# Moving w_out's first products into the attention's last steps of a two-layer encoder, with mLSTM and attention on one set of PSUM banks

## The chip, the cores and the metric

The kernel runs on one core of a Trainium2 chip. The metric is the device time of one execution in microseconds (us). TensorE does the matmuls into eight PSUM banks of 128 x 512 floats, VectorE (DVE), ScalarE (ACT) and GpSimd (POOL) the rest, and SyncE (SP) issues most DMAs.

## The reference

Two layers (`DEPTH = 2`) run over 512 rows of 1024 columns. In each layer one input projection feeds three kinds of heads side by side: eight heads of latent attention, four of a bidirectional chunked mLSTM, four of a bidirectional Mamba-2 SSD. Their outputs, put side by side, go through one output projection `w_out`, then come a layer norm, a mixture of experts (1 of 4 groups, 2 of its 4 experts a row) and a second layer norm:

```python
for l in range(DEPTH):
    p = jnp.einsum('bsd,dc->bsc', x, w_in[l])
    (c_q, c_kv, k_r, m_q, m_k, m_v, m_o, m_g, s_z, s_xbc, s_dt) = _split(p, IN_SIZES)
    y_a = _mla(c_q, c_kv, k_r, cos, sin, ...)
    y_b = _mlstm(m_q, m_k, m_v, m_o, m_g, ...)
    y_c = _ssd(s_z, s_xbc, s_dt, ...)
    heads = jnp.concatenate([y_a, y_b, y_c], -1)
    mix = jnp.einsum('bsc,cd->bsd', heads, w_out[l])
    x = _layernorm(DEEPNORM_ALPHA * x + mix, ln1_g[l], ln1_b[l])
    ffn = _hier_moe(x, ...)
    x = _layernorm(DEEPNORM_ALPHA * x + ffn, ln2_g[l], ln2_b[l])
```

The mLSTM's end matters here: its output `h` is normalised per head of 64 columns (mean, variance, inverse root) and multiplied by the sigmoid of `m_o`, the output gate.

## The kernel before, in words

All data of the run lie in 37 slots of SBUF of 128 x 1040 words (`Slots`, L100), which the code takes with `get` or, in halves, with `get_half`, and gives back with `free`. Free slots stand in a list, first in, first out. Free halves stand in one of their own: `get_half` takes the oldest free half, and cuts a new slot only where there is none; two free halves of a slot join again. Who gets which slot is settled when the program is written. An instruction that writes into a slot must wait on the chip until the last reader of that slot's former contents is done.

PSUM banks are handed out in the same way. Banks 0 to 2 (`PA`) hold projections, the attention's key and query products (`pk`, `pq`) and its outputs (`po_`). Of the other five, two belong to the mLSTM (`PM`) and three to the attention's scores and transposes (`PT_`), L253:

```python
PM, PT_ = Slots(banks[MA:MA + NM], 512), Slots(banks[NPA:MA] + banks[MA + NM:8], 512)
```

The mixing stage of a layer is a set of generators, each of which does one step when it is asked: `ssd` (d, L921, 19 steps), `projections` (p, L993), `mlstm` (m, L1066, 16 steps), `mla_in` (i, L1236), `ssd_heads` (h, L984), and the attention's `scores` (s) and `values` (v, from L1289). A head's `scores` are five steps: the q product, and a score tile with its softmax for each of four row tiles. The q product is six matmuls, a multiplication by the rotation table `rot` into a half slot (`qf`), and a split into a high and a low part. `values` are four steps of transposes, and for each second head two more with the products with v. One string, `SEQ` (L72), tells in which order the steps are asked for, a letter each. That settles the program order, and with it slots and banks. A planner then lays out each engine's queue, in program order where it can, and takes a later instruction first where by its model the earlier one isn't ready. On the chip each engine works through its queue in that order. All instructions of VectorE, ScalarE and TensorE go through one helper and carry the line L230; all loads have L277, POOL's splits L410, and POOL's normalisation of a probability tile L1338. In the trace `s` is any slot, `b` any bank, and `xt` one of the eight pairs of slots for x transposed and later for the heads' outputs.

The last two steps of `projections` are the two halves of the output gate: each is two row tiles of 24 matmuls with 256 columns, and leaves a half slot `tho`. The last step of `mlstm` does the normalisation, and its final reads of the gate free both halves:

```python
for i2 in range(2):
    hh = hb_.ap[:, i2 * 512:(i2 + 1) * 512]
    V.scalar_tensor_tensor(hh, tho[i2].ap, 1.0, hh, op0=OP.add, op1=OP.mult)
free(tho)
```

In `SEQ` the gate's halves stand before the SSD's last two steps and right behind them. `ssd_heads` (the split of the SSD heads' output) is asked for before the attention begins. The mLSTM's last step stands behind head 4's second score tile.

Behind the mixing stage comes w_out. Its weights come in eight tiles of 512 KB, four for the first 512 output columns, in the order `(3, 2, 0, 1)`: the columns of the SSD heads, of the mLSTM heads, then of the attention's. `wo_load` (L1623) loads one, `wo_split` (L1651) splits it into a high and a low part, ScalarE the one and VectorE or, for the pieces in `WOG = (0, 2)`, POOL the other. `wo_mm` (L1657) multiplies it for one row tile: six matmuls of 512 columns, 24 for the four row tiles, which add up in four banks of `P4` (banks 0 to 3). The code asks for all of it behind the attention; the planner may lay it further ahead.

Of the kernel before, what the change touches and what calls it, by code (L numbers as in the profile page):

```python
# [68 lines left out]
MA = 3  # L69
NM = 2  # L70
SSD_STEPS = 19
SEQ = 'dpddpdpdpddpdddpdpddpiddpidpiddpddphimmssmsmssmsvmsvvsmsvsmsmvssvsvvsvmmvsvsvsmvmsvsmsvmsvsvmvvsvmmsvsvsmssvvmsmsvsvmsvsvsvvssvsvvsvsvvvvvv'  # L72

ROPE_INV = [1.0, 0.5623413324356079, 0.3162277638912201, 0.17782793939113617, 0.10000000149011612,
            0.05623413249850273, 0.03162277489900589, 0.017782794311642647, 0.009999999776482582,
# [12 lines left out]
        'A n3 l2 c2 K23 Z0 o3 e3 b3 r3 r3 g3 r3 r3 l3 c3 f2 k2 K34 Z1 Z2 f3 H Z3')  # L88
WPIN = ''
NU = 7  # L90
WOG = (0, 2)
MG = (16, 16)
PTV = range(8)
GSEQ = 'gzgzgzgzzz'
# [118 lines left out]
def tile_trunk(ctx: ExitStack, tc: tile.TileContext, ins, out, dbg=None, depth=DEPTH):  # L213
# [36 lines left out]
    Q, R = View(pool, F32R), View(pool, F32)  # L250
    banks = [psp.tile([128, 512], F32, name=f"b{i}") for i in range(8)]
    PA, PB = Slots(banks[0:NPA], 512), Slots(banks[NPA:8], 512)
    PM, PT_ = Slots(banks[MA:MA + NM], 512), Slots(banks[NPA:MA] + banks[MA + NM:8], 512)  # L253
    lows_ = {}
    lastp, lows = ["pre"], {}

# [151 lines left out]
    def split(dst_h, dst_l, src, eng=V):  # L408
        r = A.activation(dst_h, src, AF.Copy)
        eng.tensor_sub(dst_l, src, dst_h.bitcast(F32))  # L410
        return r
# [147 lines left out]
    for l in range(depth):  # L559
# [361 lines left out]
        def ssd():  # L921
            for g in range(2):
                py = PB.get()
                cbs = []
                (_, ch, cl), (_, bh, bl) = cc_[g], bb_[g]
                for d in range(2):
                    bcs, bds = [], []
                    for e in range(2):
                        p = bcast(8 * d + 4 + 2 * g + e, PB)
                        bcs.append(p)  # L930
                        b = R.get_half()
                        V.tensor_tensor(b.v("p (a c) -> p a c", a=NT), p.v("p (a c) -> p a c", a=NT),
                                        (neg_u if d == 0 else neg_l)[:, None, :].to_broadcast([128, NT, 128]), op=OP.add)
                        bds.append(b)
                    for i in range(NT):
                        if d == 0:
                            pcb = PB.get()
                            s = slice(i * 128, (i + 1) * 128)
                            mm3(pcb.ap, bh[:, s], bl[:, s], ch, cl)
                            cb = R.get_half()  # L940
                            A.activation(cb.ap, pcb.ap, AF.Copy)
                            pcb.free()
                            cbs.append(cb)
                        lo_, hi_ = (i, NT) if d == 0 else (0, i + 1)
                        w = slice(lo_ * 128, hi_ * 128)
                        Ls = []
                        for e in range(2):
                            hd = 2 * g + e
                            L = R.get_half()
                            for c in range(lo_, hi_):  # L950
                                b = slice(c * 128, (c + 1) * 128)
                                src = bds[e] if c == i else bcs[e]
                                A.activation(L[:, b], src[:, b], AF.Exp, bias=sb[d][:, abs(c - i), i, hd:hd + 1])
                            V.tensor_mul(L[:, w], cbs[i][:, w], L[:, w])
                            Ls.append(L)
                        for e in range(2):
                            hd = 2 * g + e
                            T.matmul(py[64 * e:64 * e + 64, w], xdt[d][i][:, hd * 64:hd * 64 + 64], Ls[e][:, w],
                                     start=(d == 0 and i == 0), stop=(d == 1 and i == NT - 1), skip_group_check=True)
                        free(Ls)  # L960
                        yield
                    free(bcs, bds)
                free(cbs)
                y = R.get_half()
                V.scalar_tensor_tensor(y.ap, xs[g].ap, dsk[:, g:g + 1], py.ap, op0=OP.mult, op1=OP.add)
                py.free()
                V.tensor_mul(y.ap, y.ap, z2[g].ap)
                q = R.get_half()
                A.activation(q.ap, y.ap, AF.Square)
                yz.append(y)  # L970
                yq.append(q)
                free(cc_[g][0], bb_[g][0])
                yield
            free(xdb, xs, z2)
            r = rms_cols([[q.ap] for q in yq], 128.0, 4e-6)
            free(yq)
            for g in range(2):
                p = row_bc(r, g * NT)
                V.scalar_tensor_tensor(yz[g].ap, yz[g].ap, pt[:, 5 + g, 6:7], p.ap, op0=OP.mult, op1=OP.mult)
                p.free()  # L980
                tap("ssd%d_%d" % (l, g), yz[g].ap)
            yield

        def ssd_heads():  # L984
            for g in range(2):
                finish_heads(6 + g, yz[g].ap)
                yz[g].free()
            yield
# [247 lines left out]
        def mla_in():  # L1236
            for i in range(2):
                b, h, lo = pair()
                split(h[64:96], lo[64:96], kra[64:96])
                V.tensor_copy(h[96:128], h[64:96].bitcast(F32))  # L1240
                V.tensor_copy(lo[96:128], lo[64:96].bitcast(F32))
                kb.append((b, h, lo))
            kra.free()
            rq = rms_cols([[q.ap for _, q in cqb]], 256.0, 1e-6)

            qsc = small([128, 2, NT], tag="qsc")
            for c in range(2):
                V.tensor_scalar(qsc[:, c], rq, (1.0, -1.0)[c] * 96.0 ** -0.5, None, op0=OP.mult)
            qn = [c for c, _ in cqb]
            rk = rms_cols([[ckb[0][1].ap]], 128.0, 1e-6)  # L1250
            p = row_bc(rk, 0)
            c = ckb[0][0]
            V.scalar_tensor_tensor(c.ap, c.ap, pt[:, 2, 6:7], p.ap, op0=OP.mult, op1=OP.mult)
            p.free()
            kn = pair(c.ap)
            free(ckb[0][0], [b for _, b in cqb + ckb])
            yield
            ukv = R.get(1024)
            load(ukv.ap, ins["w_ukvp"], l * RANK_KV * 1024, [[1024, 128], [1, 1024]])
            uk = []  # L1260
            for w in range(2):
                b, h, lo = pair()
                split(h, lo, ukv[:, w * 512:(w + 1) * 512])
                uk.append((b, h, lo))
            ukv.free()
            yield
            vt = []
            for i in range(NT):
                s = slice(i * 128, (i + 1) * 128)
                p = PA.get()  # L1270
                mm3(p.ap, kn[1][:, s], kn[2][:, s], uk[1][1], uk[1][2])
                v = R.get_half()
                A.activation(v.ap, p.ap, AF.Copy)
                p.free()
                vt.append(v)
            uk[1][0].free()
            mla.update(qsc=qsc, qn=qn, kn=kn, uk=uk[0], vt=vt)
            router_sums()
            yield
# [110 lines left out]
                    if PHASE:  # L1390
                        print(t[2], "steps", t[0] - 1, "of", t[1])

        streams = {"d": ssd(), "p": projections(), "m": mlstm(), "i": mla_in(), "h": ssd_heads()}
        for n, t in enumerate(SEQ):
            ph({"m": "mlstm", "d": "ssd", "p": "proj"}.get(t, "attn"))
            if t == "s" and "s" not in streams:
                streams["s"], streams["v"] = attention()
            next(streams[t], 1)
        for t in "dphmisv":
            assert next(streams[t], 1) == 1  # L1400
        free([b for b, _, _ in kb], [b for b, _, _ in mla["qn"]], mla["kn"][0], mla["uk"][0], mla["vt"])


        P4, P5 = Slots(banks[0:4], 512), Slots(banks[4:8], 512)


        class Expert:
# [212 lines left out]

        ph("wout")

        def wo_load(hf, q):  # L1623
            raw = R.get(1024, full=True)
            load(raw.ap, ins["w_outp"], ((l * 2 + hf) * 4 + q) * 128 * 1024, [[1024, 128], [1, 1024]])
            return raw

        order = (3, 2, 0, 1)
        raws = [[wo_load(0, q) for q in order]]
        xr = load_x(ins["x"] if l == 0 else x2d)  # L1630
        ln1 = load_ln(1)
        lg = small([128, NT, 20], tag="lg")
# [3 lines left out]
        def ranks(a, b):  # L1636
# [10 lines left out]
            V.tensor_reduce(r1, gt4, axis=AX.X, op=OP.add)  # L1647
            V.tensor_sub(df[:, n], df[:, n], r1)
            gb_.free()

        def wo_split(raw, n):  # L1651
            h, lo = Q.get(1024, full=True), Q.get(1024, full=True)
            split(h.ap, lo.ap, raw.ap, G if n in WOG else V)
            raw.free()
            return h, lo

        def wo_mm(p, i, q, w, first, last):  # L1657
            s = slice(i * 128, (i + 1) * 128)
            for a in range(2):
                j = 2 * q + a  # L1660
                cc = slice(a * 512, a * 512 + 512)
                mm3(p.ap, xh[j][:, s], xl[j][:, s], w[0][:, cc], w[1][:, cc],
                    start=(first and a == 0), stop=(last and a == 1))

        def evac(p, i, hf):

# [19 lines left out]
            p.free()  # L1686

        lgt = [R.get_half(plain=True) for _ in range(2)]
        ps = [P4.get() for _ in range(NT)]
        for a, q in enumerate(order):  # L1690
            w = wo_split(raws[0][a], a)
            for i in range(NT):
                wo_mm(ps[i], i, q, w, a == 0, a == 3)
            free(w)
# [535 lines left out]
```

## Time and profile before

Three runs took 1066.09, 1066.67 and 1069.11 us. The profile is of one execution.

| | before |
|---|---|
| time, median of 3 runs | 1066.67 us |
| time of the profiled execution | 1070.26 us |
| span of the profiled execution | 1067.8 us |
| its mean granted TensorE clock | 0.974 |
| TensorE busy (matmuls) | 996.5 us, 93% |
| VectorE busy | 836.0 us, 78% |
| ScalarE busy | 644.6 us, 60% |
| GpSimd busy | 267.2 us, 25% |

The busy time of an engine is the sum over its instructions, its share is that of the span. The granted clock is what the chip allowed TensorE, as a share of 2.4 GHz; a stretch at 0.50 ran at 1.2 GHz. Times in views of the trace count from the start of the span. The mixing stage's part that the change touches lies from about 155 to 295 us in the first layer and from about 685 to 822 us in the second.

### The profile page before, as it was taken

Reading aid. Unit: us, or ns where it says so; the run is one execution under the profiler, and the core shown is the slowest. Engines: PE = TensorE matmul, PEld = TensorE weight load, DVE = VectorE, ACT = ScalarE, POOL = GpSimd, SP = SyncE. Lnnn points to the kernel's source line nnn. Section 1 sums busy time; section 2 is a strip of 40 time slices with the busy share of each in tenths; the row PEclk is TensorE's granted clock in tenths of the full one; section 3 lists DMA queues with packets and bytes.
Section 4 is the critical chain, followed back from the end, with each engine's and each line's share of the span. In section 5 each row is a group of like instructions: output and inputs, shape, how many; then the busy total and the mean of one; then the engine's idle time right before and its main releaser. Section 6 shows DMA issues by size and latency. Waiting matters only on the chain. (4 is left out here: it accounts for less than half of the span.)

```text
span 1067.8 us, 15553 instructions
## 1 busy us (share of the span) xinstructions
PE 996.5 (93%) x5310; PEld 739.2 (69%) x5310; DVE 836.0 (78%) x1832; ACT 644.6 (60%) x1182; POOL 267.2 (25%) x232
## 2 busy tenths in 40 slices
PE   6999999988998999999999999999799989999995
PEld 6876788555687666666598768876466876666653
DVE  8995557787749799999969955577876498999996
ACT  5565646555524588888646564466464347778874
POOL 1000002223003255565100000022220123556652
PEclk9999989998999899999999998999999989999998
DMA  7211100132656889996532120011347477999933
GB/s 305 69 45 45 40 21 21 35 126 99 234 198 218 282 288 345 335 324 213 204 139 70 40 69 1 21 40 41 118 138 246 168 275 264 311 339 337 308 94 155
DMA packets 51795, 176.76 MB, mean 166 GB/s; under 512 B 8169, under 2 KB 8681, under 8 KB 51712
## 3 DMA queue, kind: packets, MB, share of 16 engines
q1 hardware_dynamic: 45216, 160.42, 42.2%
q0 software_dynamic: 6496, 15.31, 6.0%
q8 instruction: 42, 0.69, 0.3%
q14 instruction: 41, 0.34, 0.1%
HBM read 159.61 MB, written 23.59 MB: 172 GB/s over the span
## 5 line engine op out<-in xcount | busy, mean ns | idle before, releaser
L230 PE MATMUL b<-xt,s 128*128 128x512 f32 (+3 forms) x1484 | 327.1, 367 | 13.8 <-ACT s L230 8.6
L230 PE MATMUL b<-s,s 128*128 128x512 f32 (+7 forms) x1308 | 324.7, 404 | 14.0 <-ACT s L230 7.1
L230 PEld LDWEIGHTS b<-xt,s 128*128 128x128 f32 (+2 forms) x1484 | 234.0, 183 | 80.3 <-issue 11.5
L230 DVE TENSOR_TENSOR s<-s,s 128x1024 fp32r<-128x1024 f32 (+8 forms) x254 | 247.6, 1000 | 50.5 <-ACT s L230 41.7
L230 PEld LDWEIGHTS b<-s,s 128*128 128x128 f32 (+3 forms) x1308 | 185.0, 173 | 99.7 <-DVE s L230 22.6
L230 ACT ACTIVATE s<-b 128x512 f32<-128x512 f32 (+8 forms) x282 | 135.0, 496 | 191.2 <-PE b L230 182.3
L230 ACT ACTIVATE s<-s 128x1024 fp32r<-128x1024 f32 (+5 forms) x219 | 191.6, 910 | 85.1 <-DVE s L230 31.8
L230 PE MATMUL b<-s,xt 128*128 128x256 f32 (+2 forms) x944 | 209.1, 362 | 0.4 <-POOL s L1523 0.4
L230 PEld LDWEIGHTS b<-s,xt 128*128 128x128 f32 (+1 forms) x944 | 150.6, 192 | 34.7 <-issue 4.8
L230 DVE TENSOR_TENSOR xt<-s,xt 128x1024 fp32r<-128x1024 f32 (+1 forms) x106 | 118.3, 1122 | 13.8 <-ACT xt L230 13.7
L230 ACT ACTIVATE xt<-s 128x1024 fp32r<-128x1024 f32 (+1 forms) x107 | 110.4, 1042 | 26.1 <-PE b L230 17.7
L230 PE MATMUL b<-ident,s 128*128 128x128 f32 (+3 forms) x736 | 107.4, 273 | 18.6 <-POOL s L1338 7.7
L230 PEld LDWEIGHTS b<-ident,s 128*128 128x128 f32 (+3 forms) x736 | 81.5, 153 | 53.3 <-ACT s L230 13.9
L1598 POOL DMA_INDIRECT acc<-s,slx x28 | 55.3, 1976 | 99.3 <-ACT s L230 79.4
L230 ACT ACTIVATE s<-b,mx,qsc 128x512 f32<-128x512 f32 x64 | 49.7, 782 | 25.5 <-DVE mx L230 25.1
L1338 POOL TENSOR_SCALAR s<-s,sums 128x512 f32<-128x512 f32 x48 | 37.6, 788 | 105.7 <-DVE sums L230 93.6
L1094 POOL MEMSET s<- 128x780 f32 x4 | 3.0, 756 | 219.9 <-DVE s L230 186.3
L230 DVE TENSOR_REDUCE mx<-b 128x1 f32<-128x512 f32 x64 | 43.2, 686 | 18.3 <-PE b L230 17.9
L1446 POOL DMA_INDIRECT s<-x1d,slx x30 | 40.5, 1351 | 57.4 <-PE b L230 23.0
L230 DVE TENSOR_TENSOR s<-b,s 128x192 fp32r<-128x192 f32 (+3 forms) x92 | 46.9, 524 | 4.6 <-POOL s L1127 2.6
L230 PE MATMUL b<-xt 128*96 128x512 f32 x160 | 48.0, 406 | 1.4 <-DVE xt L230 1.4
L230 ACT ACTIVATE s<-b,slw 96x512 f32<-96x512 f32 (+1 forms) x60 | 39.1, 682 | 14.9 <-PE b L230 8.3
(254 smaller groups left out, 983.9 us busy)
## 6 DMA issues: line engine op xcount, KB each, us to landing
s<-in_w_gu_dram SPq DMA_DIRECT2D x128, 512.0 KB
s<-in_expert_w_down_dram SPq DMA_DIRECT2D x64, 512.0 KB
s<-in_w_inp_dram SPq DMA_DIRECT2D x36, 512.0 KB
s<-in_w_outp_dram SPq DMA_DIRECT2D x16, 512.0 KB
x1d<-s SPq DMA_DIRECT2D x8, 512.0 KB
acc<-s SPq DMA_DIRECT2D x8, 512.0 KB
s<-acc SPq DMA_DIRECT2D x8, 512.0 KB
s<-in_x_t_dram SPq DMA_DIRECT2D x4, 512.0 KB
```

Of the source, the lines that this page charges most:

```text
L230: r = f(*a, **kw)
L1094: G.memset(cb.ap, 0.0)
L1338: (V if hd in NORMV else G).tensor_scalar(P.ap, P.ap, sums, 0.0, op0=OP.mult, op1=OP.add)
L1446: self.ga = G.indirect_dma_start(out=self.xg[:BLK], out_offset=None, in_=x1d[0:128 * n, :], in_offset=bass.IndirectOffsetOnAxis(ap=ix[:BLK ...
L1598: G.indirect_dma_start(out=acc[:, :], out_offset=bass.IndirectOffsetOnAxis(ap=self.ix[:BLK, 0:1], axis=0), in_=yt[:BLK], in_offset=None, b ...
```

## The change

The change touches the order of the mixing stage and nothing of its arithmetic, but for the engine of one subtraction.

- `SEQ` is new. The gate's two halves come behind the q product and the second score step of head 0, the split of the SSD heads' outputs (h) behind head 1's q product. The mLSTM's steps stand closer: from head 1's first score step on, one mLSTM step to each score and value step, so that its last step comes behind head 3's first score tile.
- The mLSTM and the attention's scores and transposes take their banks from one list of five.
- w_out's first two pieces, those of the SSD's and the mLSTM's heads, become a generator `wout` (w) with nine steps: the loads behind head 6's q product, then the banks and a row tile's six matmuls at a time, one step behind each of head 7's score tiles and head 6's last value steps. The split for the first piece moves from POOL to VectorE. The products add up in two banks of the first three and two of the five.
- The rest of w_out, pieces 2 and 3 and the second 512 columns, stays behind the attention. `P4` is then the four banks that the stream has taken, `P5` the other four.

```diff
-SEQ = 'dpddpdpdpddpdddpdpddpiddpidpiddpddphimmssmsmssmsvmsvvsmsvsmsmvssvsvvsvmmvsvsvsmvmsvsmsvmsvsvmvvsvmmsvsvsmssvvmsmsvsvmsvsvsvvssvsvvsvsvvvvvv'
+SEQ = ('dpddpdpdpddpdddpdpddpiddpidpidddd' 'immspsmspsmsmsh' + 'svm' * 12 + 'sv' * 13 + 'w' + 'sv' * 5
+       + 's' + 'wvs' * 4 + 'wv' * 4 + 'vv')
...
-WOG = (0, 2)
+WOG = (2,)
...
-    PM, PT_ = Slots(banks[MA:MA + NM], 512), Slots(banks[NPA:MA] + banks[MA + NM:8], 512)
+    PM = PT_ = Slots(banks[NPA:8], 512)
...
+        order = (3, 2, 0, 1)
+        raws, ps = [], []
...
+        def wout():
+
+            raws.extend(wo_load(0, q) for q in order[:2])
+            yield
+            ps.extend(p.get() for p in (PA, PA, PM, PM))
+            for a in range(2):
+                w = wo_split(raws[a], a)
+                for i in range(NT):
+                    wo_mm(ps[i], i, order[a], w, a == 0, False)
+                    yield
+                free(w)
+
-        streams = {"d": ssd(), "p": projections(), "m": mlstm(), "i": mla_in(), "h": ssd_heads()}
+        streams = {"d": ssd(), "p": projections(), "m": mlstm(), "i": mla_in(), "h": ssd_heads(), "w": wout()}
...
-        P4, P5 = Slots(banks[0:4], 512), Slots(banks[4:8], 512)
+        own = [banks.index(b.pool.tiles[b.i]) for b in ps]
+        P4, P5 = Slots([banks[n] for n in own], 512), Slots([banks[n] for n in range(8) if n not in own], 512)
+        free(ps)
+        ps = [P4.get() for _ in range(NT)]
...
-        raws = [[wo_load(0, q) for q in order]]
+        raws = [raws + [wo_load(0, q) for q in order[2:]]]
...
-        for a, q in enumerate(order):
+        for a, q in list(enumerate(order))[2:]:
             w = wo_split(raws[0][a], a)
             for i in range(NT):
                 wo_mm(ps[i], i, q, w, a == 0, a == 3)
```

`wo_load`, `wo_split` and `wo_mm` are moved ahead of the generators, unchanged.

## Rows read from the trace of the kernel before

**Rows 1.** The page, first lines: the span, and section 1 (busy microseconds of each engine, share of the span, instructions).

```profile
span 1067.8 us, 15553 instructions
...
PE 996.5 (93%) x5310; PEld 739.2 (69%) x5310; DVE 836.0 (78%) x1832; ACT 644.6 (60%) x1182; POOL 267.2 (25%) x232
```

**Rows 2.** Busy time by stretch, from the windows of the trace; first the first layer, then the second. Columns: the stretch and its length, then PE, PEld, DVE, ACT and POOL busy with their instructions, the granted TensorE clock (1.00 is 2.4 GHz, 0.50 is 1.2 GHz), the DMA engines' mean busy share, GB/s.

```profile
172.00:231.00 59.00, 56.41 (x312) 39.49 (x312) 47.11 (x132) 35.79 (x95) 16.68 (x25) 1.00 0.23 72
231.00:240.48 9.48, 6.05 (x23) 2.62 (x21) 7.97 (x20) 5.55 (x10) 1.45 (x2) 1.00 0.20 67
240.48:250.72 10.24, 7.60 (x22) 4.54 (x21) 8.71 (x18) 4.55 (x8) 5.32 (x3) 0.50 0.21 72
251.00:294.60 43.60, 42.55 (x201) 28.29 (x201) 29.91 (x62) 26.15 (x47) 5.14 (x5) 1.00 0.53 185
698.00:758.90 60.90, 56.80 (x314) 39.87 (x313) 46.97 (x132) 36.04 (x97) 16.81 (x25) 1.00 0.21 70
758.90:769.55 10.65, 5.98 (x22) 2.45 (x20) 9.17 (x21) 6.00 (x11) 2.61 (x3) 1.00 0.29 98
769.55:776.38 6.83, 5.39 (x15) 2.97 (x16) 5.47 (x13) 2.70 (x4) 2.71 (x3) 0.50 0.00 0
778.50:821.40 42.90, 41.86 (x198) 27.68 (x197) 29.34 (x63) 26.14 (x47) 5.16 (x5) 1.00 0.56 188
```

**Rows 3.** The waits of TensorE in three stretches: 231 to 251 us (the first two lines), 172 to 231 us (the next two) and 698 to 758.9 us (the last two). Columns: waiting engine, what it wrote, its line, then what released it; microseconds in all, number of waits, the mean of one.

```profile
PE b L230 <- ACT s L230: 3.8, 3, 2.1
PE b L230 <- POOL s L1338: 2.2, 1, 2.2
...
PE b L230 <- ACT s L230: 2.1, 4, 0.6
PE b L230 <- POOL s L1338: 0.2, 1, 0.2
...
PE b L230 <- ACT s L230: 2.5, 5, 0.7
PE b L230 <- POOL s L1338: 1.0, 3, 0.4
```

**Rows 4.** Time line of TensorE's matmuls (start, microseconds, engine, line, operation, out<-in, shape, count of like instructions in a row; idle time before them in brackets, where there was any), around head 5's q product of each layer and from 250 us.

```profile
227.89 2.67 PE L230 MATMUL b<-s,s 128*64 128x512 f32 x10
...
250.82 0.39 PE L230 MATMUL b<-s,xt 128*128 128x512 f32 x1
251.05 2.26 PE L230 MATMUL b<-s,s 128*128 128x512 f32 x9
253.15 2.02 PE L230 MATMUL b<-s,xt 128*128 128x512 f32 x8
...
755.58 2.67 PE L230 MATMUL b<-s,s 128*64 128x512 f32 x10
```

**Rows 5.** Time line of VectorE in the last mLSTM step, first and second layer, same columns.

```profile
241.00 1.21 DVE L230 TENSOR_TENSOR s<-s,s 128x1024 fp32r<-128x1024 f32 x1
...
245.60 1.29 DVE L230 SCALAR_TENSOR_TENSOR s<-s,s 128x512 f32<-128x512 f32 x2
246.93 0.69 DVE L230 TENSOR_TENSOR s<-b,rot 128x512 f32<-128x512 f32 x1
...
773.27 1.29 DVE L230 SCALAR_TENSOR_TENSOR s<-s,s 128x512 f32<-128x512 f32 x2
774.60 0.69 DVE L230 TENSOR_TENSOR s<-b,rot 128x512 f32<-128x512 f32 x1
```

**Rows 6.** Time line of VectorE, the same q multiplication (512 wide, by the table rot) for other heads: heads 3, 4 and 6 of the first layer, heads 6 and 7 of the second.

```profile
205.85 0.68 DVE L230 TENSOR_TENSOR s<-b,rot 128x512 f32<-128x512 f32 x1
...
223.43 0.68 DVE L230 TENSOR_TENSOR s<-b,rot 128x512 f32<-128x512 f32 x1
...
256.06 0.69 DVE L230 TENSOR_TENSOR s<-b,rot 128x512 f32<-128x512 f32 x1 [0.38 <-PE b L230]
...
782.81 0.69 DVE L230 TENSOR_TENSOR s<-b,rot 128x512 f32<-128x512 f32 x1 [0.37 <-PE b L230]
...
796.37 0.67 DVE L230 TENSOR_TENSOR s<-b,rot 128x512 f32<-128x512 f32 x1
```

**Rows 7.** Busy time by stretch of the instructions on tile xt alone, TensorE only: w_out's products in the first 20 us behind the mLSTM, first and second layer. Columns: the stretch and its length, PE busy with its instructions, granted clock, DMA share, GB/s.

```profile
250.80:270.00 19.20, 6.36 (x20) 1.00 0.40 131
777.50:797.00 19.50, 6.36 (x20) 1.00 0.46 153
```

**Rows 8.** Time lines of the first layer, the engine named in each row: TensorE at the gate projection's second half (the 48 matmuls of 256 columns) and behind it, w_out's first load on SP, and w_out's first split on ScalarE and POOL.

```profile
157.26 6.00 PE L230 MATMUL b<-s,xt 128*128 128x256 f32 x48
163.09 1.84 PE L230 MATMUL b<-ones,s 128*128 128x1 f32 x16
164.79 0.63 PE L230 MATMUL b<-ident,s 128*128 128x128 f32 x4
165.18 2.57 PE L230 MATMUL b<-s,s 128*128 128x512 f32 x11
...
188.79 0.33 SPq L277 DMA_DIRECT2D s<-in_w_outp_dram  x1
...
246.37 1.06 ACT L230 ACTIVATE s<-s 128x1024 fp32r<-128x1024 f32 x1 [1.27 <-issue]
...
247.57 2.38 POOL L410 TENSOR_TENSOR s<-s,s 128x1024 fp32r<-128x1024 f32 x1 [4.12 <-issue]
```

More of the change, by code (lines that the diff above doesn't have):

```diff
@@ L1391, in mix, with wo_load, wo_split, wo_mm @@
                         print(t[2], "steps", t[0] - 1, "of", t[1])
-        streams = {"d": ssd(), "p": projections(), "m": mlstm(), "i": mla_in(), "h": ssd_heads()}
+        order = (3, 2, 0, 1)
+        raws, ps = [], []
+        def wo_load(hf, q):
+            raw = R.get(1024, full=True)
+            load(raw.ap, ins["w_outp"], ((l * 2 + hf) * 4 + q) * 128 * 1024, [[1024, 128], [1, 1024]])
+            return raw
+        def wo_split(raw, n):
+            h, lo = Q.get(1024, full=True), Q.get(1024, full=True)
+            split(h.ap, lo.ap, raw.ap, G if n in WOG else V)
+            raw.free()
+            return h, lo
+        def wo_mm(p, i, q, w, first, last):
+            s = slice(i * 128, (i + 1) * 128)
+            for a in range(2):
+                j = 2 * q + a
+                cc = slice(a * 512, a * 512 + 512)
+                mm3(p.ap, xh[j][:, s], xl[j][:, s], w[0][:, cc], w[1][:, cc],
+                    start=(first and a == 0), stop=(last and a == 1))
+        def wout():
+            raws.extend(wo_load(0, q) for q in order[:2])
+            yield
+            ps.extend(p.get() for p in (PA, PA, PM, PM))
+            for a in range(2):
+                w = wo_split(raws[a], a)
[4 more added lines that the diff above has]
+        streams = {"d": ssd(), "p": projections(), "m": mlstm(), "i": mla_in(), "h": ssd_heads(), "w": wout()}
         for n, t in enumerate(SEQ):
@@ L1398, in tile_trunk @@
             next(streams[t], 1)
-        for t in "dphmisv":
+        for t in "dphmisvw":
             assert next(streams[t], 1) == 1
         free([b for b, _, _ in kb], [b for b, _, _ in mla["qn"]], mla["kn"][0], mla["uk"][0], mla["vt"])
-        P4, P5 = Slots(banks[0:4], 512), Slots(banks[4:8], 512)
+        own = [banks.index(b.pool.tiles[b.i]) for b in ps]
+        P4, P5 = Slots([banks[n] for n in own], 512), Slots([banks[n] for n in range(8) if n not in own], 512)
+        free(ps)
+        ps = [P4.get() for _ in range(NT)]
         class Expert:
@@ L1621, in tile_trunk @@
         ph("wout")
[L1623 to L1628, printed above, removed]
-        raws = [[wo_load(0, q) for q in order]]
+        raws = [raws + [wo_load(0, q) for q in order[2:]]]
         xr = load_x(ins["x"] if l == 0 else x2d)
@@ L1649, in ranks @@
             gb_.free()
[L1651 to L1663, printed above, removed]
         def evac(p, i, hf):
@@ L1688, in tile_trunk @@
         lgt = [R.get_half(plain=True) for _ in range(2)]
-        ps = [P4.get() for _ in range(NT)]
-        for a, q in enumerate(order):
+        for a, q in list(enumerate(order))[2:]:
             w = wo_split(raws[0][a], a)
```

## The prediction

> **What bounds the kernel now.** The page first: TensorE is busy 996.5 us of a span of 1067.8, VectorE 78% of it [rows 1]. An average says little here, so I cut each layer's mixing stage, the only stage that the edit touches, into stretches by the last mLSTM step and by the clock [rows 2]. In the first layer the matmul engine is idle 59.00 - 56.41 = 2.59 us in the stretch of mLSTM with heads 0 to 4 (172 to 231 us), and 43.60 - 42.55 = 1.05 us in the last stretch, where w_out's products already run beside heads 5 to 7. Between them lie 20 us that look different: 9.48 - 6.05 = 3.43 us idle, then 10.24 - 7.60 = 2.64 us idle at a granted clock of 0.50, the 1.2 GHz level. Work at half clock takes twice its time, so those 7.60 us hold 3.80 us of work at 2.4 GHz. Loss in this hole: 3.43 + 2.64 + 3.80 = 9.87 us. The second layer has the same hole: 10.65 - 5.98 = 4.67, 6.83 - 5.39 = 1.44, and half of 5.39 is 2.70, together 8.81 us. Both: 18.7 us.
>
> What ends the waits there? The waits [rows 3] name ScalarE and POOL; the time lines tell why these are late. Head 5's q product leaves TensorE within ten matmuls that end at 227.89 + 2.67 = 230.56 (in the second layer 755.58 + 2.67 = 758.25) [rows 4], yet its multiplication by the rotation table starts on VectorE at 246.93 [rows 5]. In between VectorE works through the last mLSTM step (mean, variance, inverse root, gate). The multiplication starts 0.04 us after that step's gate operations end (245.60 + 1.29 = 246.89). In the second layer it is 774.60 against 773.27 + 1.29 = 774.56. That is no accident of one run: counting the get and free calls of the code in order, head 5's rotated q is the fifth half slot taken after the last mLSTM step has freed its own, and it is handed the half that held the output gate, which those very operations read. So attention stands until the mLSTM chain is through, scores of head 5 follow at 251, and w_out's first split, whose slot held the gate's other half, waits too [rows 4, 8].
>
> **The change part by part.**
>
> 1. *mLSTM sooner.* The last step moves from behind head 4's second score tile to behind head 3's first, six score steps earlier. Nothing is removed: its work, a good part of VectorE's 7.97 + 8.71 us in the hole [rows 2], must still be done. What changes is who takes a half slot of the gate. Between that step and the next q multiplication (head 4) now lie six takers (three probability tiles, three transposed ones); the fifth is head 3's last probability tile, not a q. A late probability tile holds up one head's transposes, while the next head's q product and the values of head 2 can still run; a late q holds up everything. Bounds: all of the 18.7 us goes, or none. Whether a later taker is still caught I can't read from the trace, so I take the middle: 9.4 us for both layers.
>
> 2. *Five shared banks.* Attention had three, mLSTM two. In the stretch 172 to 231 TensorE waited 2.1 us in all for ScalarE and 0.2 for POOL, in the second layer 2.5 and 1.0 [rows 3]. Those are the waits which more banks could end: a gain of at most 5.8 us. Against it: the banks go round in one order, so a score tile can now get a bank that a slow mLSTM step still holds. No row shows shared banks; the nearest row for such a loss is the stretch's idle time, 2.59 and 4.10 us [rows 2], which could double. Between -5.8 and +6.7 I take 0.
>
> 3. *Gate projection later.* Its second half is 48 matmuls of 256 columns, 6.00 us [rows 8], which run from 157.26, while the SSD's last output is gated. They go behind head 0's q product. The work stays; in its old place kt's transposes and head 0's q product can run, as they did at 164.79 to 167.75 [rows 8]. Should nothing fill it, up to the 6.00 us per layer would be waited out twice over; the SSD's norm (16 one-column matmuls, 1.84 us) follows at once, so I take 0. The later SSD heads cost two splits on engines that aren't full: 0.
>
> 4. *w_out's first two pieces as a stream.* 48 products per layer. A run of 8 took 2.02 us [rows 4], 0.25 each, so 12 us. They are moved, not removed, and before they already filled: 20 of them ran from 250.8 to 270 and TensorE was idle hardly at all there [rows 2, 7]. Now they are asked for only after head 7's q product, so heads 3 to 6 must keep TensorE busy by themselves. Can they? From head 5 to head 6 the q multiplications lie 256.06 - 246.93 = 9.13 us apart [rows 5, 6], in the second layer 782.81 - 774.60 = 8.21, with some w_out products among them; with mLSTM they lie 17.6 and 23.5 us apart. So attention alone runs at 8 to 9 us a head when nothing holds it. I cost the loss at 0, its far end is rival D. The four loads per layer move past other loads on SP's queue: the first now stands at 188.79 on SP's own time line, 58 us ahead of its split at 246.37 [rows 8]; in the new place two are asked for a head ahead of their splits. 0.
>
> 5. *The first split on VectorE instead of POOL.* 1.21 us there in place of 2.38 [rows 5, 8]. VectorE is busy 29.91 of 43.60 us in the last stretch. 0.
>
> After the attention nothing is changed; the stages behind start earlier, and their loads wait for slots which the same end frees. If they took back half, 4.7 us would be left.
>
> Sum: 9.4 us less. On the profiled execution 1070.26 - 9.4 = 1060.9; that execution lies 3.6 above the median of the runs, 1066.67, so the forecast for the median is **1057.3 us**.
>
> **The rivals.**
>
> *B, the hole closes altogether* (no taker is caught): 1066.67 - 18.7 = 1048. For it: nothing but the slot ties the two chains together. Against: VectorE was busy 7.97 of 9.48 us in the hole, and the mLSTM work is now packed more densely.
>
> *C, the hole only moves*: a gate half is still taken by something that the attention needs, and it stands as long. Then the change does not do what it says: 1066.7.
>
> *D, slower: a bare middle.* If attention is caught as before and the stretch between the last mLSTM step and head 7 has no filler, the 20 products that ran beside heads 5 and 6 (5.0 us a layer) find no gap and are added behind: 1066.7 + 10 = 1077. It decides at a head's spacing: above some 9 us a head TensorE has holes. The second layer's 13.6 us from head 6 to head 7 (796.37 - 782.81) [rows 6] speaks for it, but there w_out's products held TensorE, not the attention.
>
> *E, the queue of TensorE.* In the last stretch no wait of TensorE stands before a w_out product [rows 4]: they were placed when bank and split were there. If a product now stands ahead of the attention's work and waits for its split, 1.06 + 1.21 us [rows 5, 8] pass with all behind it held. Four pieces: 9.1 us, which eats the forecast: 1066.4. The Trainium skill, PSUM — Partial Sum Buffer, section Engine vs sequencer instructions, says of this that the other engines' queues are strict FIFO and that matmuls start in program order; by that rule a product in the stream is no longer a pure filler. [...]
>
> **How the numbers follow.** Forecast 0.45 (own range 1050 to 1063), B 0.12, C 0.17, D 0.18, E 0.08. A measurement of this kernel can tell 0.3%, 3.2 us, from no change. Faster than 1063.5: nearly all of the forecast, B and a little of C, 0.56. Slower than 1069.9: D and the upper edges of C and E, 0.26. The rest, 0.18, is between. The range holds forecast, B, C, E and the lower part of D: 1045 to 1074. The bounds of parts 1 and 2 together, 18.7 + 5.8, would give 1042; that end I leave out.
>
> **What the profile after would show.** Step 1 right: no stretch at clock 0.50 between 170 and 300 us, and a q multiplication never more than 2 us behind the matmuls that feed it, except in the shorter stall. Wrong: again some 6 us of idle TensorE per layer, with a probability or q operation starting right at the end of the gate's. Step 2: waits for ScalarE ahead of score matmuls of 1 us and more vanish. Step 4: q multiplications of heads 4 to 6 about 9 us apart; 12 or more would make D right. Step 3: idle TensorE around 157 to 165 would make it wrong. The whole is wrong if the time saved in the mixing stage is not found at the kernel's end, or if the hole is gone and the time has not moved.

## The result and the profile after

The changed kernel takes 1079.33 us, the median of four runs (1077.92 to 1081.39), against 1066.38 for the kernel before beside it: a ratio of 1.0124, 95% interval 1.0091 to 1.0157. It is 13 us slower; the forecast was 9.4 us less. The profiled execution took 1081.39 us. Its page, first lines, as [rows 1] (the helper's line L230 is L231 in the changed kernel, POOL's L1338 is L1339):

```profile
span 1079.4 us, 15555 instructions
...
PE 997.2 (92%) x5310; PEld 744.3 (69%) x5310; DVE 836.2 (77%) x1834; ACT 645.4 (60%) x1182; POOL 262.5 (24%) x230
```

TensorE does the same work (997.2 against 996.5 us busy) in a span that is 11.6 us longer, so the loss is idle time. To see where, I measured the stage that the change touches from one landmark to another, both in every kernel: from the end of the value projection to the start of w_out's fourth piece. In the windows of the kernel before these are (columns as in [rows 2]):

```profile
153.40:294.60 141.20, 131.49 (x680) 91.15 (x679) 103.20 (x256) 80.39 (x175) 29.34 (x35) 0.96 0.29 98
679.20:821.40 142.20, 130.96 (x679) 90.83 (x678) 102.61 (x255) 80.56 (x175) 29.29 (x35) 0.98 0.29 97
```

and in the changed kernel the same two, then the first layer's in three parts and the second layer's hole:

```profile
150.30:298.00 147.70, 131.57 (x679) 94.23 (x679) 100.97 (x256) 79.98 (x175) 26.54 (x34) 0.93 0.28 96
684.80:833.50 148.70, 132.20 (x679) 94.99 (x678) 102.14 (x255) 80.60 (x175) 26.63 (x34) 0.93 0.28 96
150.30:221.00 70.70, 66.84 (x388) 51.49 (x388) 50.13 (x142) 40.39 (x100) 15.29 (x22) 0.98 0.12 38
221.00:245.00 24.00, 13.63 (x52) 8.98 (x50) 18.12 (x41) 7.87 (x15) 3.66 (x4) 0.65 0.32 111
245.00:298.00 53.00, 51.09 (x244) 33.76 (x243) 32.72 (x75) 31.72 (x61) 7.59 (x8) 1.00 0.48 168
756.30:780.30 24.00, 13.42 (x52) 9.02 (x51) 18.08 (x40) 7.92 (x15) 3.68 (x4) 0.67 0.31 109
```

The stage got 6.5 us longer in either layer, 13.0 together, which is the whole difference (11.6 us between the two profiled spans); idle TensorE grew from 9.71 to 16.13 us and from 11.24 to 16.50. The hole that the prediction saw in 20 us [rows 2] is still there, and deeper: the row from 221 to 245 says 24.00 - 13.63 = 10.37 us idle, against 3.43 + 2.64 = 6.07 before, and the second layer's 24.00 - 13.42 = 10.58 against 4.67 + 1.44 = 6.11. The rest of the loss is 1.3 us ahead of the hole in the first layer (3.86 idle to 221) and 0.9 behind it in either layer.

What TensorE waits for from 225 to 245 us, by its waits (columns as in [rows 3]):

```profile
PE b L231 <- DVE s L231: 4.9, 2, 3.2
PE b L231 <- POOL s L1339: 2.9, 2, 1.8
PE b L231 <- ACT s L231: 1.9, 2, 1.4
```

Its time line there (as [rows 4]):

```profile
225.02 0.66 PE L231 MATMUL b<-ident,s 128*128 128x128 f32 x4 [1.44 <-ACT s L231]
226.73 0.55 PE L231 MATMUL b<-ident,s 128*128 128x128 f32 x3 [1.06 <-POOL s L1339]
227.72 1.16 PE L231 MATMUL b<-s,s 128*128 128x512 f32 x3 [0.44 <-ACT s L231]
230.69 0.69 PE L231 MATMUL b<-ident,s 128*128 128x128 f32 x2 [1.81 <-POOL s L1339]
234.58 2.15 PE L231 MATMUL b<-ident,s 128*128 128x128 f32 x8 [3.21 <-DVE s L231]
237.44 1.12 PE L231 MATMUL b<-ident,s 128*128 128x128 f32 x4 [0.71 <-DVE xt L231]
238.29 1.65 PE L231 MATMUL b<-s,s 128*128 128x512 f32 x3
```

and VectorE over the same time:

```profile
222.67 1.21 DVE L231 TENSOR_REDUCE mu<-s 128x16 f32<-128x1024 f32 x1
...
226.51 1.23 DVE L231 TENSOR_TENSOR s<-s,s 128x1024 fp32r<-128x1024 f32 x1
...
228.87 1.20 DVE L231 TENSOR_TENSOR s<-s,s 128x1024 fp32r<-128x1024 f32 x1
...
232.58 1.22 DVE L231 TENSOR_TENSOR s<-s,rq_y 128x1024 f32<-128x1024 f32 x1
233.84 1.29 DVE L231 SCALAR_TENSOR_TENSOR s<-s,s 128x512 f32<-128x512 f32 x2
236.63 1.60 DVE L231 SCALAR_TENSOR_TENSOR xt<-b,pth,xt 128x512 fp32r<-128x512 f32 x2 [1.50 <-ACT xt L231]
...
245.33 0.69 DVE L231 TENSOR_TENSOR s<-b,rot 128x512 f32<-128x512 f32 x1 [0.23 <-PE b L231]
...
257.29 0.69 DVE L231 TENSOR_TENSOR s<-b,rot 128x512 f32<-128x512 f32 x1
```

At 234.58 TensorE starts the eight transposes of the last mLSTM step, after 3.21 us of waiting for VectorE, whose two gate operations of that step run from 233.84 to 233.84 + 1.29 = 235.13 (each writes one half, and the first transposes need only the first half). Only behind them come four transposes for head 2 (237.44) and head 3's last score tile (238.29). The four wait 0.71 us for VectorE's operation on `xt` that starts at 236.63, and that operation is the one which reads the mLSTM's transposes out of their bank. The q product of head 5 left TensorE by 222.17 + 1.41 = 223.58 at the latest; its multiplication is at 245.33, 22 us later. Before it was 16 us [rows 4, 5]. Head 6's follows at 257.29, 12 us behind.

The calls in the code tell why these two groups stand behind the mLSTM. The five shared banks go round: after the last step has asked for its two (banks 5 and 6, in the order of the program), the next five requests get banks 7, 3, 4, 5 and 6. The fourth is head 2's transposes, the fifth head 3's last score tile. They can't be written before the mLSTM's transposes have been read, and these stand at the end of a chain on VectorE (mean at 222.67, gate at 233.84) that takes over 12 us.

Counted in the same way, the slot tie of the prediction is gone in the first layer of this kernel: both slots of the gate become whole again, and no half slot of the attention is cut from them. Head 5's q takes a half slot that held head 3's first probability tile instead, which head 3's transposes have to read first, and its row (245.33) names TensorE as what it waited for.

### The profile page after: what moved, and what is told of

The parts are those of the page before. It is cut to its first block, busy times and chain, and to the rows that moved or that the text cites. A ratio compares the mean times of both kernels' runs of the same rounds, so it can differ in the third digit from the quotient of the medians.

```text
span 1079.4 us, 15555 instructions
## 1 busy us (share of the span) xinstructions
PE 997.2 (92%) x5310; PEld 744.3 (69%) x5310; DVE 836.2 (77%) x1834; ACT 645.4 (60%) x1182; POOL 262.5 (24%) x230
## 5 line engine op out<-in xcount | busy, mean ns | idle before, releaser
L231 PE MATMUL b<-s,s 128*128 128x512 f32 (+8 forms) x1300 | 331.4, 407 | 12.3 <-DVE s L231 10.0
L231 PE MATMUL b<-xt,s 128*128 128x512 f32 (+3 forms) x1484 | 326.4, 366 | 15.9 <-ACT s L231 9.2
L231 DVE TENSOR_TENSOR s<-s,s 128x1024 fp32r<-128x1024 f32 (+5 forms) x256 | 250.5, 1003 | 52.0 <-ACT s L231 45.5
L231 PEld LDWEIGHTS b<-xt,s 128*128 128x128 f32 (+2 forms) x1484 | 233.3, 183 | 82.9 <-issue 11.7
L231 PEld LDWEIGHTS b<-s,s 128*128 128x128 f32 (+3 forms) x1300 | 187.9, 175 | 103.6 <-DVE s L231 29.5
L231 ACT ACTIVATE s<-b 128x512 f32<-128x512 f32 (+8 forms) x282 | 135.8, 496 | 196.7 <-PE b L231 188.1
L231 ACT ACTIVATE s<-s 128x1024 fp32r<-128x1024 f32 (+5 forms) x219 | 191.3, 909 | 87.2 <-DVE s L231 36.0
L231 PE MATMUL b<-s,xt 128*128 128x256 f32 (+2 forms) x944 | 204.1, 357 | 0.5 <-POOL s L1562 0.4
L231 PEld LDWEIGHTS b<-s,xt 128*128 128x128 f32 (+1 forms) x944 | 147.9, 186 | 32.5 <-issue 3.2
L231 PE MATMUL b<-ident,s 128*128 128x128 f32 (+3 forms) x736 | 107.5, 279 | 28.1 <-DVE s L231 11.7
L231 DVE TENSOR_TENSOR xt<-s,xt 128x1024 fp32r<-128x1024 f32 (+1 forms) x106 | 120.5, 1141 | 16.5 <-ACT xt L231 16.5
L231 ACT ACTIVATE xt<-s 128x1024 fp32r<-128x1024 f32 (+1 forms) x107 | 110.4, 1042 | 26.7 <-PE b L231 20.9
L231 PEld LDWEIGHTS b<-ident,s 128*128 128x128 f32 (+3 forms) x736 | 84.8, 157 | 54.4 <-POOL s L1339 17.2
L231 ACT ACTIVATE s<-b,mx,qsc 128x512 f32<-128x512 f32 x64 | 49.7, 781 | 28.4 <-DVE mx L231 23.2
L1339 POOL TENSOR_SCALAR s<-s,sums 128x512 f32<-128x512 f32 x48 | 35.8, 751 | 112.1 <-DVE sums L231 99.5
L231 DVE TENSOR_REDUCE mx<-b 128x1 f32<-128x512 f32 x64 | 42.8, 685 | 19.0 <-PE b L231 18.7
L231 DVE TENSOR_TENSOR s<-b,s 128x192 fp32r<-128x192 f32 (+3 forms) x92 | 47.2, 525 | 7.5 <-PE b L231 5.0
L231 PE MATMUL b<-xt 128*96 128x512 f32 x160 | 47.8, 405 | 1.4 <-DVE xt L231 1.4
L231 ACT ACTIVATE s<-b,slw 96x512 f32<-96x512 f32 (+1 forms) x60 | 38.9, 682 | 15.4 <-PE b L231 8.1
```

Source lines behind the costliest of these rows:

```text
L231: r = f(*a, **kw)
L1339: (V if hd in NORMV else G).tensor_scalar(P.ap, P.ap, sums, 0.0, op0=OP.mult, op1=OP.add)
```

## The experiments

Theories. **Banks:** the last mLSTM step holds two of five shared banks through its VectorE chain, and attention queues behind it. **Packing:** the mLSTM is too close among the heads and VectorE is loaded with w_out's splits there. **Stream:** w_out's products are missing as filler in the middle, the prediction's rival D. All runs at a glance; the last column is the stage between the two landmarks, both layers together, from each run's profile.

| kernel | us, median | ratio to before (95%) | stage, us |
|---|---|---|---|
| before | 1066.38 | | 283.4 |
| changed | 1079.33 | 1.0124 (1.0091 to 1.0157) | 296.4 |
| e1 changed, banks apart | 1062.76 | 0.9967 (0.9949 to 0.9984) | 279.1 |
| e2 before, banks shared | 1073.24 | 1.0059 (1.0032 to 1.0086) | 288.6 |
| e3 changed, last banks late (7) | 1059.56 | 0.9937 (0.9910 to 0.9964) | 278.4 |
| e5 before, gate kept | 1068.41 | 1.0037 (1.0013 to 1.0060) | 283.8 |
| e6 e1 without the stream | 1066.85 | 1.0010 (0.9987 to 1.0034) | 283.6 |
| e7 e1, gate projection early | 1069.01 | 1.0021 (0.9999 to 1.0044) | 284.4 |
| e8 e1, last step late (7) | 1062.24 | 0.9970 (0.9956 to 0.9985) | 278.9 |
| e9 e3, splits on POOL | 1063.79 | 0.9980 (0.9964 to 0.9996) | 278.8 |
| e10 e2, last banks late | 1077.54 | 1.0108 (1.0076 to 1.0139) | 294.5 |
| e11 before, gate freed after head 5's q | 1068.01 | 1.0028 (1.0014 to 1.0043) | 282.5 |
| e12 changed, last banks late (11) | 1057.94 | 0.9919 (0.9892 to 0.9946) | 273.0 |
| e13 e10, gate freed after head 5's q | 1069.70 | 1.0031 (1.0010 to 1.0052) | 281.9 |
| e14 e12 without the stream | 1060.98 | 0.9960 (0.9942 to 0.9978) | 277.1 |

The kernel before beside them had medians of 1065.57 to 1065.88. The intervals are 3 to 7 us wide, so a difference of 2 us between two kernels is not told from none. The stage is of one execution each, whose own time can lie some us off the median (1070.26 us for the kernel before, against 1066.38).

### Whose banks (e1, e2, e3, e12)

e1 gives the mLSTM its own two banks back and leaves everything else of the change:

```diff
-    PM = PT_ = Slots(banks[NPA:8], 512)
+    PM, PT_ = Slots(banks[MA:MA + NM], 512), Slots(banks[NPA:MA] + banks[MA + NM:8], 512)
```

> The changed kernel with one part undone: the mLSTM again has two banks of its own, attention three. Bank theory: in the changed kernel the last mLSTM step takes two of the five shared banks in program order (banks 5 and 6) long before its VectorE chain is through, and head 3's last score tile and transposes queue behind them; with banks apart TensorE's idle time in the hole (10.4 us of 24 in the first layer) falls back to the 6.1 us of before or less, and the time to 1068 us or less. Packing theory (the closer mLSTM order and two splits on VectorE in the middle of its last step are what costs): 1076 us or more. Stream theory (w_out's products are missing as filler in the middle): 1076 us or more as well.

Measured: 1062.76 us, 16.6 less than the changed kernel and below the kernel before, as the bank theory said. Its hole by the windows:

```profile
221.00:245.00 24.00, 20.11 (x82) 12.16 (x81) 21.24 (x54) 12.05 (x26) 6.33 (x8) 0.86 0.29 95
```

and TensorE's waits in it:

```profile
PE b L231 <- ACT s L231: 3.7, 3, 2.3
PE b L231 <- DVE s L231: 0.2, 1, 0.2
```

Idle are 24.00 - 20.11 = 3.89 us instead of 10.37, and TensorE waits 0.2 us for VectorE instead of 4.9. What waits are left are for ScalarE. Head 5's q multiplication is hardly earlier than in the changed kernel (245.33), on VectorE's time line:

```profile
244.79 0.67 DVE L231 TENSOR_TENSOR s<-b,rot 128x512 f32<-128x512 f32 x1
```

So the 16.6 us don't hang on when head 5 starts. What differs is what TensorE gets done before that: 82 matmuls in the 24 us instead of 52. e2 does the opposite edit to the kernel before (the same two lines, the other way round).

> The kernel before with one part of the change alone: mLSTM and attention share five banks, order as before. Bank theory: the last mLSTM step stands behind head 4's second score tile and will hold two banks through its chain here as well, so the hole of 20 us gets 3 to 5 us more idle time a layer: 1072 to 1077 us. Packing and stream theory: shared banks cost nothing by themselves, 1063 to 1068 us.

Measured: 1073.24, inside what the bank theory gave. Its hole by the windows:

```profile
231.00:251.00 20.00, 10.80 (x40) 6.53 (x39) 18.40 (x42) 9.99 (x18) 5.14 (x5) 0.76 0.23 75
```

and the longest wait in it, on TensorE's time line:

```profile
246.39 2.15 PE L230 MATMUL b<-ident,s 128*128 128x128 f32 x8 [7.42 <-DVE s L230]
```

One wait of 7.42 us stands ahead of the last step's transposes; idle are 9.20 us of 20, against 6.07 before. e3 keeps the banks shared and cuts the last step in two, so that the two banks are asked for when its chain is nearly through:

```diff
             free(tho)
+            yield
             tap("mlstm%d" % l, hb_.ap)
...
-'svm' * 12 + 'sv' * 13 + 'w'
+'svm' * 11 + 'sv' * 7 + 'm' + 'sv' * 7 + 'w'
```

> The changed kernel, with the last mLSTM step cut in two: normalisation and gate where they were, its transposes (which take the two banks) seven score steps later. Nothing is added. Bank theory: no score tile waits for a bank of the mLSTM any more; the time falls at least as far as with banks apart, to 1055 to 1068 us. Packing or stream theory: 1076 us or more.

Measured: 1059.56, 19.8 us less than the changed kernel by two lines that move no work off any engine. e12 asks eleven score steps later instead of seven.

> The changed kernel with the last step's transposes eleven score steps later instead of seven (1059.6). Bank theory: once the banks are taken behind the end of the VectorE chain, more delay is worth nothing: 1057 to 1062 us. If the gain came from where the transposes run and not from the banks: more than 3 us away from 1059.6.

Measured: 1057.94, as expected, and the best of all: 0.8% faster than the kernel before. Its hole and the stretch behind it in the first layer, and both of the second:

```profile
219.00:243.00 24.00, 21.18 (x93) 12.69 (x92) 20.96 (x54) 13.62 (x30) 8.46 (x8) 0.93 0.37 127
243.00:286.90 43.90, 43.51 (x207) 29.21 (x206) 30.07 (x66) 26.90 (x50) 5.15 (x5) 1.00 0.55 194
743.50:767.50 24.00, 20.88 (x93) 12.23 (x92) 20.94 (x56) 13.60 (x29) 8.46 (x8) 0.93 0.38 126
767.50:811.70 44.20, 43.81 (x207) 29.39 (x207) 30.52 (x66) 27.54 (x51) 5.16 (x5) 1.00 0.53 194
```

Idle are 2.82 us in the 24, and 0.39 in the 43.90 behind it. Two edits that take the tie away end the loss, and the one that puts it into the old order brings a loss there too: in the new order the bank theory holds, and packing and stream, which e1 and e3 leave in place, don't explain the loss. Why the same tie costs 16.6 us in the new order and 7.4 in the old is not settled.

### Is sharing bad as such (e8, e10, e13)

e8 is e3 with banks apart.

> Banks apart and the last mLSTM step's transposes seven score steps later. Bank theory in its strict form: sharing five banks is harmful by the last step alone, so with that step cut it is free or a gain; then this kernel is not faster than the one that shares five banks and has the late transposes (1059.6): 1059 to 1064 us. If sharing costs at every mLSTM step: 1052 to 1057 us.

Measured: 1062.24. With the last step's banks asked for late, sharing five is not worse; it is 2.7 us better (1059.56), which the two intervals, as they overlap, don't tell from none. By e1 against e8 the late step alone is worth nothing where the banks are apart. Both are what the strict bank theory said. The Trainium skill, Perfetto Trace Analysis, section Matmul Optimizations, asks for all eight PSUM banks to be used for parallelism. All kernels here use all eight, so no run tests that. What cost the changed kernel 16.6 us was two banks of a shared list, held by a step that had nothing to put into them yet. e10 tried the same in the order of before: e2's shared banks, the same `yield`, and three of the letters m taken out of `SEQ`, so that the second half comes six score steps later.

> The kernel before with five shared banks (1073.2 alone), and the transposes of the last mLSTM step six score steps later. Bank theory: the loss of the shared banks goes in the old order as well, 1060 to 1067 us. If sharing costs in another way in this order (earlier mLSTM steps): 1071 to 1075.

A miss: 1077.54, slower than e2. In its trace no long wait stands ahead of the mLSTM's transposes any more. What is left is the other tie, the one that the prediction had read. Head 5's q multiplication on VectorE, and TensorE waiting for what follows from it:

```profile
244.25 1.29 DVE L230 SCALAR_TENSOR_TENSOR s<-s,s 128x512 f32<-128x512 f32 x2
247.27 0.69 DVE L230 COPY s<-b 128x512 f32<-128x512 f32 x1 [1.73 <-PE b L230]
247.88 0.68 DVE L230 TENSOR_TENSOR s<-b,rot 128x512 f32<-128x512 f32 x1
...
248.61 1.65 PE L230 MATMUL b<-s,s 128*128 128x512 f32 x3 [1.45 <-DVE s L230]
```

In the old order head 5's q still takes the gate's half slot, whose last reads start at 244.25 and take 1.29 us; behind them stands one copy, for which VectorE waits 1.73 us for TensorE. Why e10 is slower than e2, which has both ties, no run shows. e13 therefore frees the gate behind head 5's q step as well (edit as in e11 below).

> The kernel before with five shared banks, the last mLSTM step's transposes late (1077.5 with these two), and in addition the gate's halves freed behind head 5's q step. Two-tie theory: in the old order both the slot and the two banks tie head 5 to the last mLSTM step, and a run that cuts one leaves the other; with both cut 1056 to 1066 us. If the old order costs in another way once banks are shared: 1070 us or more.

Measured: 1069.70, 7.8 less than e10, and neither of the two values expected. The slot was a tie there (7.8 us), but with both cut the old order is no better than the kernel before. So the late banks pay in the new order alone, and what holds the old one is open; by the row, VectorE is busy for 89% of the stretch:

```profile
229.00:249.00 20.00, 14.91 (x64) 9.26 (x63) 17.85 (x50) 12.00 (x23) 5.70 (x6) 0.91 0.29 92
```

### The prediction's own hole (e5, e11)

e5 is the kernel before with `free(tho)` moved behind the attention, so that no half slot is cut from the gate; e11 moves it only behind head 5's q step:

```diff
-            free(tho)
             tap("mlstm%d" % l, hb_.ap)
...
             next(streams[t], 1)
+            if t == 's' and SEQ[:n].count('s') == 25:
+                free(tho)
```

> The kernel before, but the two half slots of the output gate are freed behind the attention and not in the last mLSTM step, so that no later half slot is cut from them; one slot less for the rest of the stage. Slot theory (the prediction's reading of the hole): head 5's q multiplication no longer waits for the gate's last reads, the stretch at clock 0.50 near 240 us vanishes, and 9 to 19 us go: 1048 to 1058 us. If the slot was only one tie of several (banks, VectorE's own order): the hole stays within 3 us of its size and the time within 1063 to 1068 us.

> The kernel before, but the gate's two halves are freed right behind head 5's q step instead of in the last mLSTM step: the q multiplication is free of the gate, and the slot is missing for three score steps only, not to the end of the stage. If the kept slot ate the gain of the run that kept it (1068.4): 1050 to 1060 us. If the slot was never what the hole hangs on, since VectorE has 17 us of work in 20 there: 1063 to 1069 us.

Measured: 1068.41, just above its second range, and 1068.01, in its second: no gain in either, and by the intervals a small loss. In e5 the q multiplication came free, as the reading of the slot said, and the hole got shallower (VectorE's time line, then the windows of the hole and of the rest):

```profile
229.14 0.69 DVE L230 TENSOR_TENSOR s<-b,rot 128x512 f32<-128x512 f32 x1 [0.24 <-PE b L230]
```

```profile
229.00:249.00 20.00, 15.99 (x63) 9.46 (x62) 16.79 (x42) 11.47 (x21) 6.50 (x7) 0.83 0.18 54
249.00:292.80 43.80, 41.53 (x186) 26.05 (x185) 29.45 (x56) 23.68 (x43) 5.22 (x4) 1.00 0.54 182
```

It starts at 229.14 instead of 246.93 [rows 5]. But VectorE was busy 7.97 + 8.71 = 16.68 of 19.72 us in the hole before [rows 2] and is busy 16.79 of 20.00 now. TensorE's idle time there went from 6.07 to 4.01 us, and 1.2 of these 2.1 us came back in the last stretch (43.80 - 41.53 = 2.27 us idle against 1.05). The tie was real, and cutting it gained nothing. The row points to VectorE as what is late next; no run tested that by itself. Nor did the attention stand still in that hole before the change: between the operations of the mLSTM VectorE took maxima of score tiles there, as in

```profile
237.31 0.69 DVE L230 TENSOR_REDUCE mx<-b 128x1 f32<-128x512 f32 x1 [0.80 <-PE b L230]
...
239.24 0.68 DVE L230 TENSOR_REDUCE mx<-b 128x1 f32<-128x512 f32 x1
```

### The other parts (e6, e7, e9, e14)

e6 is e1 without the stream: the letters w out of `SEQ`, w_out's products and the first split on POOL as before.

> The changed order of mLSTM and gate projection alone: banks apart as before, no stream of w_out (all its pieces are asked for behind the attention, the first split on POOL, as before). It differs from the run with banks apart (1062.8) by the stream. If the stream takes filler away from the middle (rival D in small): this one is 3 us or more faster, 1054 to 1060. If the stream itself brings the gain that is left with banks apart: 1066 us or more, as before. If neither: 1061 to 1065.

Measured: 1066.85, as before within the interval, and 4.1 us more than e1: the second answer. e14 takes the stream out of e12.

> The best version so far (1057.9: changed order, shared banks, the last step's transposes eleven score steps later), without the stream of w_out's first pieces. With banks apart the stream was worth 4.1 us (1066.9 against 1062.8). If it is worth as much here: 1060 to 1064 us; if the stream's worth was tied to the banks: 1056 to 1059.

Measured: 1060.98, 3.0 more than e12; the first answer. The stream is worth 3 to 4 us either way, though each difference is about as wide as its interval. Both runs also put the first split back on POOL, and e9 below puts 4.2 us on the engine of two splits; so the 3 to 4 us may be the split's and not the products', and no run separates them. e7 puts the gate's two halves and the SSD heads' split back to their old places in e1.

```diff
-'dpddpdpdpddpdddpdpddpiddpidpidddd' 'immspsmspsmsmsh'
+'dpddpdpdpddpdddpdpddpiddpidpiddpddph' 'immssmssmsms'
```

> The changed kernel with banks apart, and the gate projection and the SSD heads' split back in their old places (the mLSTM's steps one score step later by it, at most). Against the run with banks apart (1062.8): if the later gate projection is worth nothing, as the prediction took it, 1061 to 1065 us; if it hides the end of the SSD and gives, 1065 to 1072; if it costs (the attention starts later for it), below 1060.

Measured: 1069.01, in the second range, with runs from 1062 to 1072. The later gate projection, together with the later split of the SSD heads, is worth some 6 us in this order, by the medians. e9 puts the first two splits on POOL in e3 (`WOG = (0, 1, 2)`).

> Five shared banks, the last step's transposes late (1059.6), and the splits of w_out's first two pieces on POOL and not on VectorE, where they fell between the operations of the last mLSTM step (2.4 us a layer). If VectorE's queue in that step is now what ends last: 2 to 5 us faster, 1054 to 1058. If not: 1058 to 1062.

A miss on the other side: 1063.79, 4.2 us slower than e3. The splits on VectorE in the middle of the last step are not what costs; on POOL each takes about twice as long (2.38 against 1.21 us [rows 5, 8]) on the engine that also normalises the heads' probability tiles.

## Why the prediction was wrong

- **Part 2, five shared banks, taken at 0,** is the step that failed. It measured +16.6 us (changed against e1), and +7.4 in the old order (e2). The bound, +6.7, was taken from the idle time of the stretch of heads 0 to 4, where no bank was shared. The price came from the longest holder: the last mLSTM step, whose chain takes over 12 us and which is handed its two banks in program order, long before it has something to put into them. The mechanism stood in the text (a score tile gets a bank that a slow mLSTM step still holds); place and price were not looked for. They could be counted from the calls, as the half slots were.
- **Part 1, mLSTM sooner, 9.4 us of 18.7.** With banks apart and no stream, the new order (with the later gate projection) gave 1.2 us more, which the interval doesn't tell from none (e6); as the later gate projection gave 6 in e7, the mLSTM's order alone may have cost that much, but no run has it alone. The reading of the slot in the kernel before was right: in e5 the q multiplication is free at 229.14. The step from the tie to its price was wrong: the whole hole was put on one wait, though the rows showed VectorE busy for 16.68 of 19.72 us there, some of it for the attention, which did not stand until the mLSTM's chain was through. The count of the takers behind the change was wrong as well: the fifth, head 3's last probability tile, gets another half slot, and none of the attention's gets the gate's.
- **The loss put on the clock**, 3.80 and 2.70 us of the 18.7, did not show as busy time when the low stretches grew (last section). Idle time made 11.7 of the 13.0 us of the stage.
- **Part 3, gate projection later, taken at 0:** some 6 us gained, the later SSD split included (e7 against e1).
- **Part 4, the stream, taken at 0 with a loss of 10 at its far end:** 3 to 4 us gained, the first split's move to VectorE included.
- **Part 5, split on VectorE, taken at 0:** for both splits together 4.2 us better than on POOL (e9 against e3).
- **Rival D** gave 1077, 2 us from the result, by the wrong cause: without the stream e1 and e12 get slower, not faster (e6, e14); the changed kernel itself was not run without it. The sign named for it, q multiplications of heads 5 and 6 over 9 us apart, did show (257.29 after 245.33), but the jam of the banks makes the same sign. **Rival E** is not it either, by the same two runs: the stream costs nothing there. **C**, the hole only moves, was nearest in kind: it moved from a slot to a bank, and grew; but what took it over was no half of the gate.
- What the parts other than the banks give together, e1's 3.1 us, or 7.8 with the banks' tie cut in e12, is the gain that the forecast put on part 1.

## What to carry to other kernels

Where a list of buffers is shared, look for the user that holds one longest between asking and releasing: here it set the cost of sharing. Ask for the buffer where the chain that fills it ends, in a step of its own: here two lines turned 1.2% slower into 0.8% faster. It is no sure gain: the like edit in the old order gave 1077.54 us against 1073.24 (e10, e2). And before a hole is booked as the gain of cutting one tie, look at the engine behind the tie: here it was busy for five sixths of the hole, and cutting the tie gained nothing.

## What was not expected of the hardware

More time at the low clock hardly showed in TensorE's busy time. By the stage's granted clock, 0.93 of 147.70 us, the changed kernel spent (1 - 0.93) x 2 x 147.70 = 20.7 us of the first layer's stage at 1.2 GHz and 20.8 of the second's (the clock has two places, so either may be 1.5 us off); the kernel before had stretches of 10.24 and 6.83 [rows 2]. By the prediction's rule that half of the busy time at the low level is lost, the 10.5 and 14.0 us more should have cost 10.5 x 0.57 / 2 = 3.0 and 4.0 us (an estimate; 0.57 is TensorE's busy share of the hole, 13.63 of 24.00). The busy sums rose by 0.08 and 1.24 us, with the same number of matmuls. What made up for it no run shows. Where e12 closes the hole, 3.4 us at 1.2 GHz are left in it (0.93 of 24 us), against the 10.24 and 6.83 of before. But the low level also shows ahead of the hole there (0.98 of the 68.50 us from 150.50 to 219.00), where the kernel before had 1.00 [rows 2], so that by the stage's 0.97 and 0.98 some 8.2 and 5.5 us are left in all.
